# Recurrence products of a hybrid two-layer block on Trainium2: grouped by the array's form, with zero-padded 128-row operands for scores, low-rank parts and gate rows

## The chip, the cores and the metric

The kernel runs on one core of a Trainium2 chip. The metric is the device time of one execution in microseconds (us), lower is better. Engines are named as in the profile: PE is TensorE (matmuls), PEld its weight loads, DVE is VectorE, ACT is ScalarE, POOL is GpSimd, and SP issues DMAs.

## What is computed

Two layers with the same structure work on 512 tokens of width 1024: 256 context tokens and 256 latent ones. Each layer is a half-weight SwiGLU feed-forward part, a mixing part, and another feed-forward part, each behind a modulated norm. The mixing part has three branches, whose outputs are gated, projected and summed:

```python
z = h @ W_in                      # one projection, columns split among the branches
y_m = mLSTM(...)                  # 4 heads, 64-wide q and k: scores q k^T times exp(decay), both directions
y_r = RWKV7(...)                  # 8 heads of 64 channels, both directions
y_a = differential_attention(...) # 4 heads, each with two 64-wide q/k maps
x  += gate2 * W_o(sum_b sigmoid(g_b) * (y_b @ P_b))
```

The recurrent branch (RWKV-7) keeps a 64x64 state per head and direction. With decay w, removal a, key k, value v and read-out r, the state goes through S <- S diag(w) + (S a) b^T + v k^T at each token, and y = S r. The kernel computes it in chunks of 64 tokens. Within a chunk the values u of the removal term solve a triangular system, (I - A) u = X, where X has a part from the values of the chunk (Ma times v) and a part from the state (S a).

## The kernel before

Tokens lie on the free axis of feature-major tiles; a matmul works on 128 features and up to 512 tokens. Weights come from DRAM as 512 KB units (`unit`, L130), which ACT and DVE split into a leading and a trailing half (`hi`, `lo`), and each dense product is the sum of three passes, seen in the rows as `hh,hi`, `hl,hi` and `hh,lo`. Their PSUM tiles are called `m` and `d`.

The mixing part of a layer interleaves two programs. The recurrent branch runs at high priority in four tiles t = 0 to 3 of two heads each. For each tile there is `rwkv_stage1` (elementwise work and the low-rank products `lora`, L904 to 910), `rwkv_stage2` (the products A inside the chunks, L976 to 980, and transposes), `rwkv_solve` (the inverses: a chain on DVE and 32x32 products sG and sB on PE) and `rwkv_chain` (L1090 to 1161). The other program is the generator `mixers`: attention (`attn_rot`, `attn_head`), the mLSTM (`mlstm_steps`) and the merge, whose dense products fill PE between the recurrent steps. Tables (`BUDGET`, `GATES`) say how much of it goes between the columns of the recurrent tiles. The order of instructions on each engine is set when the program is built, by a scheduler that looks at priorities and at when operands are ready. PSUM has eight banks in four tags: two for `d`, three for `m` (scores too), two for `c` (the recurrent products A, X, U, S, Y) and one for `s` (low-rank products).

The chain takes eight steps. Each handles one forward and one backward chunk (d = 0, 1) of two heads (h = 0, 1), head h on partitions 64h to 64h + 63. In a step: X is four products of Ma with UV and four of ar with the state S (L1102 to 1107); DVE copies X; U is four products with the inverses Bt (L1116); DVE and ACT copy U into UV; the new state's S is four products of BK with UV (L1128), and DVE adds and scales it (L1157, L1158); and Y, by `out()` one step later, is four pairs of a product of UV with Mr and one of the state with ar (L1135 to 1137), which DVE adds to `ry` or ACT copies there. Steps i = 1 to 7 have the state products, except where both chunks are context chunks in layer 1, whose Y isn't needed.

By its operands a matmul uses a part of the array, and the profile prints that after its operands. The local product of Y (UV with Mr) contracts 128 rows into 64 columns: 128\*64. The state product (S with ar) contracts the 64 rows of a head: 64\*64. A (L980), the attention scores (L592), the mLSTM's scores (L746) and the trailing parts of the low-rank weights (L907) contract 64 rows into 128 columns: 64\*128. For the scores, two heads' or two maps' 64 features share a 128-partition tile `qkT` or `mqk`, and each product takes its half of it.

The mLSTM's gate rows lie in two 64-row tiles, `gi` and `Fc`, each with four transposes of 64 rows (L705 to 708).

Of the kernel before, what the change touches and what calls it, by code (L numbers as in the profile page):

```python
# [35 lines left out]
# columns of the packed per-partition parameters  # L36
# [3 lines left out]
# columns of the packed constants  # L40
# [10 lines left out]
# per layer: gate tiles after each attention and mLSTM head; other work (in us of TensorE) before and after  # L51
# the columns of each next recurrent tile
# [24 lines left out]
SPLIT = 16  # L77

class Halves:
    """a unit's 1024 columns in two tiles"""
# [9 lines left out]
class Builder:  # L92
# [36 lines left out]
    def unit(self, spec):  # L129
        """hi and lo parts of a unit; exact together"""  # L130
# [31 lines left out]
    def fm_tile(self, spec, lo=0, h=None, ps=None):  # L162
        """one feature-major tile of 128 columns: PSUM [128 cols, tokens]"""
# [17 lines left out]
    def fm_first(self, units, pss, parts):  # L181
        """the first tiles after a norm: every feature block goes to all of them as soon as it is there"""
# [25 lines left out]
    def ada_first(self, i, j):  # L208
        """block j of modulation vector i (0 shift, 1 scale) of the first norm, on TensorE"""
# [18 lines left out]
    def ada_first_shift(self, j):  # L228
        """the shift on VectorE"""
# [13 lines left out]
    def load_c(self, after=lambda: None):  # L243
        """silu of the two condition vectors on every partition"""
# [23 lines left out]
    def ada_steps(self):  # L268
        """the others on VectorE: one block of 128 outputs at a time"""
# [27 lines left out]
    def sqrt_ahead(self):  # L297
        """has ScalarE's table for the square roots of the next norm loaded before they are due"""
# [4 lines left out]
    def sumsq(self, k, c):  # L303
        """adds the squares of x_k to the running sum of these tokens"""
# [9 lines left out]
    def norm_stats(self, parts):  # L314
        """1 / rms of these tokens on every partition, in PSUM"""
# [16 lines left out]
    def norm_apply(self, l, i, k, psr, parts):  # L332
        """feature block k of the modulated norm, split into hi and lo"""
# [12 lines left out]
    def norm_mod(self, l, i, parts):  # L346
        """norm and modulation of these tokens"""
# [5 lines left out]
    def x_update(self, l, gi, k, ps, c):  # L353
        """x_k += 0.5 * gate * ps"""
# [75 lines left out]
    def conv(self, out, ps, w, lo=0):  # L430
        """out = centred 3-tap convolution of ps; w: three [128,1] taps"""
# [11 lines left out]
    def attn_prep(self):  # L443
# [21 lines left out]
        self.qg, self.nl, self.subw = qg, nl, sub  # L465

    def tm_group(self, cols, consume, t0=0):
        """token-major product with 256 columns (cols: (c0, width) ranges): PSUM [128 tokens, 256]
        for each of the token tiles from t0 on"""
# [19 lines left out]
    def attn_qk(self, h):  # L489
        """raw q and k of a head, token-major (token tile, q or k), and the sums of their squares"""  # L490
# [14 lines left out]
    def attn_qk_pair(self, hp):  # L505
        """the same for two heads without the context's q: slots k0 k1 q2 k2 q3 k3 of the token tiles"""
# [32 lines left out]
    def attn_rot(self, qkr, ss):  # L539
        """normalised and rotated q and k of a head, feature-major"""  # L540
# [29 lines left out]
        for w in range(2):  # L570
# [4 lines left out]
            o = a.tile([P, NT], F32, name="qkT", tag="qkT", bufs=4)  # L575
            nc.scalar.copy(o[:, t0 * P :], pt[:, t0 * P :])
# [3 lines left out]
    def attn_head(self, hp, h, qT, kT, v):  # L580
# [3 lines left out]
        for i in range(lo // P, 4):  # L584
# [60 lines left out]
    def mlstm_steps(self):  # L645
# [4 lines left out]
        def qk(c0, ti, lo):  # L650
# [5 lines left out]
            o = a.tile([P, NT], F32, name="mqk", tag="mqk", bufs=4)  # L656
            nc.vector.scalar_tensor_tensor(o[:, lo:], th[:, lo:], 1.0, z[:, lo:], op0=ALU.add, op1=ALU.mult)
            return o

        q, k = [], []  # L660
# [3 lines left out]
        for i in range(2):  # L664
            k.append(qk(O_MK + P * i, 2 + i, 0))
            yield 5
# [3 lines left out]
        gi = a.tile([64, NT], F32, name="gi", tag="P00", bufs=1)  # L670
# [24 lines left out]
        # m = F + G; em = exp(-m); nG = -G, its hi part on the first half of the partitions, lo on the other  # L695
        nc.vector.tensor_tensor(Fc, Fc, G, op=ALU.add)
# [7 lines left out]
        for t in range(4):  # L704
            self.tr(pt[:, t * 64 : t * 64 + 64], gi[:, t * P : (t + 1) * P], 64)  # L705
        for t in range(4):
            self.tr(pt[:, 256 + t * 64 : 256 + t * 64 + 64], Fc[:, t * P : (t + 1) * P], 64)
        used = lambda x: x.rearrange("p (t d r) -> p (t d) r", t=4, d=2)[:, :, 0:4]
        nc.scalar.copy(ac.rearrange("p t (d r) -> p (t d) r", d=2), used(pt[:, :256]))
        nc.scalar.activation(em.rearrange("p t (d r) -> p (t d) r", d=2), used(pt[:, 256:]), AF.Exp, scale=-1.0)  # L710
# [5 lines left out]
        for h in range(4):  # L716
            if h % 2 == 0:
# [9 lines left out]
                yield 10  # L727
            ps = self.fm_tile(self.blocks("w_in", l, O_MO + h * P), lo)
            tho = a.tile([P, NT], F32, name="tho", tag="tho", bufs=1)
            nc.scalar.activation(tho[:, lo:], ps[:, lo:], AF.Tanh, scale=0.5)  # L730
            r = slice(64 * (h % 2), 64 * (h % 2) + 64)
            qt, kt = q[h // 2], k[h // 2]
            # s-block j: scores against the query tokens it can reach
# [9 lines left out]
            for j in range(4):  # L743
                s0 = max(lo, 0 if j < 2 else CTX)
                pS = self.psm("mS")
                self.mm(pS[:, s0:], kt[r, j * P : (j + 1) * P], qt[r, s0:], True, True)  # L746
                for d in range(2):
                    # reachable query blocks
# [66 lines left out]
    def rwkv_small(self):  # L815
# [6 lines left out]
        # hi and lo parts of a direction on the two halves of the partitions  # L822
# [4 lines left out]
        for src, dst in ((tw, self.tw), (pa, self.ta)):  # L827
            for d in range(2):
                r, o = slice(64 * d, 64 * d + 64), slice(64 - 64 * d, 128 - 64 * d)
                nc.scalar.copy(dst[r, d], src[r])  # L830
                nc.vector.tensor_tensor(dst[o, d], src[r], dst[r, d].bitcast(F32), op=ALU.subtract)
        self.vpad = a.tile([P, 128 + NT], F32, name="vpad", tag="vpad", bufs=1)
# [22 lines left out]
    def rwkv_cols(self, t):  # L855
# [12 lines left out]
        ll = a.tile([P, 2, P], F32R, name="loral", tag="loral", bufs=1)  # L868
        nc.scalar.copy(lh, lw)
        for d in range(2):  # L870
            r = slice(64 * d, 64 * d + 64)
            nc.vector.tensor_tensor(ll[r], lw[r, d::2], lh[r, d::2].bitcast(F32), op=ALU.subtract)
# [9 lines left out]
    def rwkv_stage1(self, t, r, k, v, lw, g2):  # L882
        """everything that is elementwise over (channel, token)"""
# [5 lines left out]
        # normalised keys  # L889
# [5 lines left out]
        # 1 / max(norm, 1e-12)  # L895
# [7 lines left out]
        for d in range(2):  # L903
            rows = slice(64 * d, 64 * d + 64)  # L904
# [663 lines left out]
```

## Time and profile before

| what | value |
|---|---|
| time, median of 3 runs | 2867.44 us (2856.05 to 2876.06) |
| profiled execution: span, the one time that the page gives of it | 2880.2 us |
| PE busy | 2784.9 us, 97% |
| DVE busy | 1862.6 us, 65% |
| ACT busy | 1146.1 us, 40% |
| POOL busy | 236.5 us, 8% |
| mixing stage of layer 0 | about 430 to 1195 us |
| mixing stage of layer 1 | about 2040 to 2600 us |

Busy time is the time in which at least one instruction of the engine is under way. On PE successive matmuls overlap, so in a timeline the cost of a piece is read from its start to the next piece's start, not from its own duration. A float32 product leaves two records, a transpose or a product of split halves one. The granted clock (PEclk) is a share of full speed.

### The profile page before, as it was taken

The page shows a single profiled execution, that of the slowest core. Times are in us where ns is not written, and L with a number is a line of the kernel's source. Part 1 is how long each engine was busy: PE and PEld are TensorE (multiplying, and loading weights), DVE is VectorE, ACT ScalarE, POOL GpSimd, SP SyncE. Part 2 cuts the span into 40 slices and gives each one's busy share as a digit, 9 for nine tenths or more (in the row PEclk, how much of TensorE's full clock was granted, in tenths as well). Part 3 has the DMA queues.
Part 4 walks back from the last instruction along what each step waited for, and adds up shares of the span by engine and source line. Part 5 has one row for each costly group of instructions (what it writes and reads, how often), then busy time and mean ns, then how long its engine had stood idle before and what let it go on. Part 6 is the DMA issues. An engine that isn't in the chain of part 4 may idle for free.

```text
span 2880.2 us, 43519 instructions
## 1 busy us (share of the span) xinstructions
PE 2784.9 (97%) x17198; PEld 2280.8 (79%) x17198; DVE 1862.6 (65%) x3611; ACT 1146.1 (40%) x1955; POOL 236.5 (8%) x330
## 2 busy tenths in 40 slices
PE   7999999999999999999999999999999899998999
PEld 5888887668676677688888888888878677878999
DVE  7999368474593663589995443333877677746654
ACT  3322244443553543343222332222554546444543
POOL 0000002111110200200000000000212121112000
PEclk9999999799997999999999999999989899989999
DMA  7777322111121222666773232222221121226454
GB/s 264 237 238 227 100 94 68 34 63 39 59 75 41 70 74 80 225 205 221 237 240 109 88 102 96 95 95 74 98 78 57 61 65 57 92 92 214 162 183 147
DMA packets 102432, 349.65 MB, mean 121 GB/s; under 512 B 13362, under 2 KB 17842, under 8 KB 101972
## 3 DMA queue, kind: packets, MB, share of 16 engines
q1 hardware_dynamic: 91872, 315.10, 33.5%
q0 software_dynamic: 9024, 31.60, 3.3%
q8 instruction: 135, 2.21, 0.3%
q14 instruction: 69, 0.57, 0.1%
q10 hardware_dynamic: 1332, 0.18, 0.0%
HBM read 327.82 MB, written 19.01 MB: 120 GB/s over the span
## 4 chain that ended last, share of the span: by engine, by line
PE 60%; DVE 8%; issue 4%; ACT 3%; DMA 2%; POOL 1%; DVEq 0%; POOLq 0%; ACTq 0%; SPq 0%
PE d L102 25%; PE m L102 22%; PE Y L102 2%; PE A L102 2%; DVE lo L144 1%; PE X L102 1%; DVE op L1038 1%; DVE T L1041 1%; DMA yin<-yd 1%; DMA raw<-in_ws 1%; PE mo L102 1%; PE aS L102 1%; PE S L102 1%; PE U L1116 1%; ACT hi L140 1%
## 5 line engine op out<-in xcount | busy, mean ns | idle before, releaser
L140 ACT CAST hi<-raw 128x1024 fp32r<-128x1024 f32 x430 | 451.0, 1049 | 1022.0 <-PE m L102 468.0
L144 DVE TENSOR_TENSOR lo<-raw,hi 128x1024 fp32r<-128x1024 f32 (+1 forms) x508 | 544.6, 1076 | 322.7 <-ACT hi L140 315.6
L102 PE MATMUL m<-hh,hi 128*128 128x512 f32 (+1 forms) x1440 | 510.8, 357 | 3.9 <-ACT hh L342 2.5
L102 PE MATMUL m<-hl,hi 128*128 128x512 f32 (+1 forms) x1440 | 513.2, 357 | 0.0
L102 PE MATMUL m<-hh,lo 128*128 128x512 f32 (+1 forms) x1440 | 512.5, 357 | 0.0
L102 PE MATMUL d<-hh,hi 128*128 128x256 f32 (+1 forms) x976 | 357.5, 367 | 4.0 <-DVE x L359 2.7
L102 PE MATMUL d<-hl,hi 128*128 128x256 f32 (+1 forms) x976 | 353.1, 362 | 0.4 <-DVE hl L196 0.4
L102 PE MATMUL d<-hh,lo 128*128 128x256 f32 (+1 forms) x976 | 349.1, 358 | 0.1
L239 DVE SCALAR_TENSOR_TENSOR ajunk<-araw,scb 128x1024 f32<-128x1024 f32 x272 | 332.5, 1222 | 5.1 <-ACT scb L266 0.5
L102 PEld LDWEIGHTS m<-hh,hi 128*128 128x128 f32 x1440 | 272.0, 190 | 45.3 <-ACT hh L342 3.1
L102 PEld LDWEIGHTS m<-hh,lo 128*128 128x128 f32 x1440 | 272.8, 190 | 40.2 <-DVE lo L144 0.2
L102 PEld LDWEIGHTS m<-hl,hi 128*128 128x128 f32 x1440 | 272.8, 190 | 39.9 <-issue 0.2
L102 PE MATMUL d<-ul,hi 128*128 128x512 f32 (+1 forms) x770 | 269.3, 350 | 0.0
L102 PE MATMUL d<-uh,hi 128*128 128x512 f32 (+1 forms) x770 | 268.5, 349 | 0.0
L102 PE MATMUL d<-uh,lo 128*128 128x512 f32 (+1 forms) x770 | 268.3, 349 | 0.0
L102 PEld LDWEIGHTS d<-hh,hi 128*128 128x128 f32 x976 | 191.9, 197 | 37.5 <-issue 8.2
L102 PEld LDWEIGHTS d<-hl,hi 128*128 128x128 f32 x976 | 191.7, 196 | 34.5 <-issue 12.7
L102 PEld LDWEIGHTS d<-hh,lo 128*128 128x128 f32 x976 | 191.9, 197 | 26.3 <-issue 5.1
L102 PEld LDWEIGHTS d<-uh,hi 128*128 128x128 f32 x770 | 145.1, 188 | 20.8
L102 PEld LDWEIGHTS d<-ul,hi 128*128 128x128 f32 x770 | 145.4, 189 | 19.7
L102 PEld LDWEIGHTS d<-uh,lo 128*128 128x128 f32 x770 | 144.9, 188 | 19.9
L102 PE MATMUL d<-lo,hh 128*128 128x256 f32 x480 | 142.9, 298 | 0.0
(357 smaller groups left out, 4268.3 us busy)
## 6 DMA issues: line engine op xcount, KB each, us to landing
raw<-in_ws SPq DMA_DIRECT2D x430, 512.0 KB, 3.4
araw<-in_ws SPq DMA_DIRECT2D x146, 512.0 KB, 4.4
gd<-gth POOLq DMA_DIRECT2D x24, 256.0 KB, 2.5
gth<-gd SPq DMA_DIRECT2D x24, 256.0 KB, 2.9
xd<-x POOLq DMA_DIRECT2D x2, 2048.0 KB, 7.9
gd<-gth POOLq DMA_DIRECT2D x24, 128.0 KB, 2.0
gth<-gd SPq DMA_DIRECT2D x24, 128.0 KB, 3.3
yin<-yd POOLq DMA_DIRECT2D x11, 256.0 KB, 4.6
```

Of the source, the lines that this page charges most:

```text
L102: self.nc.tensor.matmul(out, lhsT=lhsT, rhs=rhs, start=start, stop=stop)
L140: self.nc.scalar.copy(hi, raw)
L144: self.nc.vector.tensor_tensor(lo[:, c], raw[:, c], hi[:, c].bitcast(F32), op=ALU.subtract)
L239: self.nc.vector.scalar_tensor_tensor(junk, raw, 1.0, self.scb[:, st], op0=ALU.mult, op1=ALU.mult, accum_out=self.mods[l][:, s, k, st : st ...
L1038: nc.vector.tensor_tensor(w, A[:, i + 1 :, i : i + 1].broadcast_to(w.shape), T[:, i : i + 1, c].broadcast_to(w.shape), op=ALU.mult)
L1041: nc.vector.tensor_tensor(t, t, w, op=ALU.add)
L1116: self.nc.tensor.matmul(pu[ur, d * 64 : d * 64 + 64], lhsT=Bt[hr, 8 * d + cs[d]], rhs=X[hr, d], start=True, stop=True, tile_position=(hr.s ...
```

## The change

The diff does six things.

1. Attention scores: q of a head goes into `qz`, a tile with a slot of 512 columns for each of the two maps; the other map's 64 rows are zeros, set once per layer on POOL. Each score contracts 128 rows. ACT copies q in two halves instead of one piece. `qkT` has 2 buffers instead of 4, `qz` one.
2. The mLSTM's k likewise goes into `mkz`, of which there is one; it is filled by two half-tile operations on DVE, and the second pair of heads gets its k when it is due, no longer at the start.
3. The gate rows lie in one 128-row tile `gf`, with four 128x128 transposes per layer instead of eight of 64 rows.
4. The trailing parts of the low-rank weights lie in a tile with zeros in the other direction's rows, and the product contracts 128 rows.
5. A: both heads' banks are allocated together, and the source alternates heads.
6. The chain: in X the state products of both heads come first, then the UV products. Y gets a bank in `c` for d = 0 and the bank of `s` for d = 1. Its four local products follow S directly, and its four state products with the evacuation are issued together after the X of the next step (`y_state`).

The core of the diff (comments that go and unchanged lines are left out):

```diff
@@ attn_rot
-            o = a.tile([P, NT], F32, name="qkT", tag="qkT", bufs=4)
-            nc.scalar.copy(o[:, t0 * P :], pt[:, t0 * P :])
+            if w == 0:
+                o = self.qz[self.nq % QZ[l]]
+                self.nq += 1
+                for m in range(2):
+                    mr = slice(64 * m, 64 * m + 64)
+                    nc.scalar.copy(o[mr, m, t0 * P :], pt[mr, t0 * P :])
+            else:
+                o = a.tile([P, NT], F32, name="qkT", tag="qkT", bufs=2)
+                nc.scalar.copy(o, pt)
@@ attn_head
-                r = slice(64 * m, 64 * m + 64)
-                self.mm(pS[:, : nk * P], qT[r, i * P : (i + 1) * P], kT[r, : nk * P], True, True)
+                self.mm(pS[:, : nk * P], qT[:, m, i * P : (i + 1) * P], kT[:, : nk * P], True, True)
@@ rwkv_stage1, lora
-                self.mm(ps, lw[1][rows, i], x[rows, d], False, True)
+                self.mm(ps, lw[1][:, 2 * i + d], x[:, d], False, True)
@@ rwkv_stage2
+                pAs = [self.psc("A") for _ in range(2)]
+                for n in range(4):
+                    c = 4 * g + n
+                    for h in range(2):
+                        hr = slice(64 * h, 64 * h + 64)
+                        self.mm(pAs[h][:, n * P : (n + 1) * P], bk[hr, c].rearrange("p a b -> p (a b)"),
+                                ar[hr, d, c].rearrange("p a b -> p (a b)"), True, True)
@@ rwkv_chain
+        def y_state(py, cs, S):
+            if S is not None:
+                for d in range(2):
+                    for h in range(2):
+                        hr = slice(64 * h, 64 * h + 64)
+                        self.mm(py[d][hr, :64], S[hr, d], ar[hr, d, cs[d], 1], False, True)
...
                 c = cs[d]
+                if i:
+                    for h in range(2):
+                        hr = slice(64 * h, 64 * h + 64)
+                        self.mm(px[hr, d * 64 : d * 64 + 64], ar[hr, d, c, 0], S[hr, d], True, False)
                 for h in range(2):
                     hr = slice(64 * h, 64 * h + 64)
-                    self.mm(px[hr, d * 64 : d * 64 + 64], Ma[hr, d, c], UV[hr, c, h], True, i == 0)
-                    if i:
-                        self.mm(px[hr, d * 64 : d * 64 + 64], ar[hr, d, c, 0], S[hr, d], False, True)
+                    self.mm(px[hr, d * 64 : d * 64 + 64], Ma[hr, d, c], UV[hr, c, h], i == 0, True)
...
-                py = self.psc("Y")
+                py = [self.psc("Y"), self.pss("Y")]
                 for d in range(2):
                     for h in range(2):
                         hr = slice(64 * h, 64 * h + 64)
-                        self.mm(py[hr, d * 64 : d * 64 + 64], UV[:, c, h], Mr[:, d, c, h], True, i == 0)
-                        if i:
-                            self.mm(py[hr, d * 64 : d * 64 + 64], S[hr, d], ar[hr, d, c, 1], False, True)
+                        self.mm(py[d][hr, :64], UV[:, cs[d], h], Mr[:, d, cs[d], h], True, i == 0)
```

How the order of instructions moves is shown at three places. First PE, in a step of the chain near the end of layer 0's mixing part (t = 3). U, S, X and Y are the recurrent products and d is dense filler. The rows of before:

```order
L102 MATMUL S<-UV,BK 64x64 x4
L102 MATMUL X<-UV,Ma 64x64
L102 MATMUL d<-hl,hi 128x512
L102 MATMUL d<-hh,lo 128x512
L102 MATMUL Y<-Mr,UV 64x64
L102 MATMUL Y<-ar,S 64x64
L102 MATMUL X<-S,ar 64x64
...
L102 MATMUL Y<-Mr,UV 64x64
L102 MATMUL Y<-ar,S 64x64
L102 MATMUL d<-hh,hi 128x512
L1116 MATMUL U<-X,Bt 64x64 x4
```

The rows of the change at the same place:

```order
L1161 MATMUL U<-X,Bt 64x64 x4
L103 MATMUL d<-hh,hi 128x512
L103 MATMUL d<-hl,hi 128x512
L103 MATMUL d<-hh,lo 128x512
L103 MATMUL S<-UV,BK 64x64 x4
L103 MATMUL Y<-Mr,UV 64x64 x4
L103 MATMUL Y<-ar,S 64x64 x4
L103 MATMUL d<-hh,hi 128x512
L103 MATMUL X<-S,ar 64x64 x2
L103 MATMUL X<-UV,Ma 64x64 x2
L103 MATMUL X<-S,ar 64x64 x2
L103 MATMUL X<-UV,Ma 64x64 x2
```

Before, a lone X product stood behind S, and Y's pairs stood between X and U; now X is in one piece, and Y stands ahead of it, in two runs.

Second PE at products A of one tile in layer 0, with the numbers of the buffers: A_5458 and A_5466 are the banks of head 0 and head 1. Before:

```order
L102 MATMUL A_5458<-ar_5451,bk_4674 128x128 x4
L102 MATMUL d_4985<-hh_99,lo_4982 128x512
L102 MATMUL d_4985<-hh_99,hi_4981 128x512
L102 MATMUL d_4985<-hl_100,hi_4981 128x512
...
L102 MATMUL A_5466<-ar_5451,bk_4674 128x128 x4
```

The same place in the change, where A_5468 and A_5469 are the two banks:

```order
L103 MATMUL A_5468<-ar_5461,bk_4684 128x128 x4
L106 MATMUL qkT_4865<-idt_73,qkr_4733 128x128 x2
L106 MATMUL qkT_4872<-idt_73,qkr_4733 128x128 x2
L103 MATMUL d_5029<-hh_99,lo_5026 128x512
L103 MATMUL d_5029<-hh_99,hi_5025 128x512
...
L103 MATMUL A_5469<-ar_5461,bk_4684 128x128 x4
```

The heads still stand in runs of four products of one head, though the source alternates them.

Third DVE, in the chain: S is the state, `ry` the sum of Y. Before:

```order
L1157 TENSOR_TENSOR S<-S 128x128
L1158 TENSOR_TENSOR S<-S,eC 128x128
L1111 COPY X<-X 128x128
L1143 TENSOR_TENSOR ry<-ry,Y 128x64 x2
L1121 COPY UV<-U 64x2x64
```

One of the steps in the change where the order differs most:

```order
L1193 TENSOR_TENSOR S<-S 128x128
L1134 TENSOR_TENSOR ry<-ry,Y 128x64
L1194 TENSOR_TENSOR S<-S,eC 128x128
L1134 TENSOR_TENSOR ry<-ry,Y 128x64
L604 TENSOR_REDUCE mx<-aS 128x1
L1156 COPY X<-X 128x128
```

An addition of Y stands between the two operations of the state here; in most steps both additions stand behind them.

## Rows read from the trace of the kernel before

**Rows 1.** Page, part 1: engine, busy us (share of span), instructions.
```profile
PE 2784.9 (97%) x17198; PEld 2280.8 (79%) x17198; DVE 1862.6 (65%) x3611; ACT 1146.1 (40%) x1955; POOL 236.5 (8%) x330
```

**Rows 2.** Windows by stage: busy us by engine, then PEclk, DMA share, GB/s.
```profile
430.00:1195.00 765.00, 734.37 (x4814) 549.15 (x4813) 458.69 (x1034) 334.55 (x660) 104.61 (x132) 0.93 0.21 69
...
2040.00:2600.00 560.00, 537.01 (x4234) 434.84 (x4233) 394.54 (x965) 284.65 (x552) 93.51 (x133) 0.92 0.23 73
```

**Rows 3.** Windows of the five low-clock stretches: the longest, and their sum.
```profile
871.10:908.50 37.40, 37.40 (x258) 24.05 (x258) 9.33 (x29) 12.88 (x39) 0.68 (x2) 0.50 0.07 22
...
sum 129.30, PE 129.30 PEld 89.93 DVE 34.23 ACT 49.70 POOL 5.95; mean PE 25.86 PEld 17.99 DVE 6.85 ACT 9.94 POOL 1.19
```

**Rows 4.** Timeline of PE, start of the longest one: start us, us, engine, operation.
```profile
871.05 0.90 PE L1067 MATMUL sG<-Rt,Z 32*32 32x32 f32 x13
```

**Rows 5.** Timeline of PE around a low-rank product, layer 0.
```profile
775.43 0.39 PE L102 MATMUL d<-hl,hi 128*128 128x512 f32 x1
775.66 0.40 PE L102 MATMUL lw<-tws,lorah 128*128 128x512 f32 x1
775.98 0.50 PE L102 MATMUL lw<-tws,loral 64*128 64x512 f32 x1
776.42 0.44 PE L105 MATMUL amT<-idt,ae 128*128 128x128 f32 x2
```

**Rows 6.** Timeline of PE, a chain step of layer 0's last tile.
```profile
1084.63 0.45 PE L1116 MATMUL U<-X,Bt 64*64 64x64 f32 x8
...
1085.91 0.45 PE L102 MATMUL S<-UV,BK 128*64 128x64 f32 x8
1086.29 0.33 PE L102 MATMUL X<-UV,Ma 64*64 64x64 f32 x2
1086.55 0.50 PE L102 MATMUL d<-hl,hi 128*128 128x512 f32 x1
...
1087.47 0.27 PE L102 MATMUL Y<-ar,S 64*64 64x64 f32 x1
...
1088.13 0.33 PE L102 MATMUL Y<-Mr,UV 128*64 128x64 f32 x2
...
1089.67 0.51 PE L102 MATMUL d<-hh,hi 128*128 128x512 f32 x1
1090.10 0.45 PE L1116 MATMUL U<-X,Bt 64*64 64x64 f32 x8
```

**Rows 7.** Groups by line and form, PE: busy us, mean ns, idle before.
```profile
L102 PE MATMUL Y<-ar,S 64*64 64x64 f32 x352 | 57.6, 244 | 0.0
```

**Rows 8.** Timeline of PE: a lone score, two adjacent ones, a full-row float32 product.
```profile
726.57 1.12 PE L102 MATMUL aS<-qkT 64*128 64x512 f32 x2
727.62 0.71 PE L102 MATMUL ay<-am,av 128*128 128x128 f32 x4
...
2250.45 1.13 PE L102 MATMUL aS<-qkT 64*128 64x512 f32 x4
2251.51 0.38 PE L102 MATMUL d<-hl,hi 128*128 128x256 f32 x1
...
787.14 1.02 PE L102 MATMUL gm<-ry,cst 128*128 128x512 f32 x2
...
788.23 0.39 PE L102 MATMUL d<-hl,hi 128*128 128x512 f32 x1
```

**Rows 9.** Timeline of PE, products A of both heads in one run, layer 0.
```profile
619.96 1.71 PE L102 MATMUL A<-ar,bk 64*128 64x128 f32 x16
```

**Rows 10.** Timeline of DVE in the chain step of rows 6.
```profile
1086.73 0.29 DVE L1158 TENSOR_TENSOR S<-S,eC 128x128 f32<-128x128 f32 x1
1088.23 0.29 DVE L1111 COPY X<-X 128x128 f32<-128x128 f32 x1 [1.21 <-PE X L102]
1089.77 0.35 DVE L1143 TENSOR_TENSOR ry<-ry,Y 128x64 f32<-128x64 f32 x2 [1.25 <-PE Y L102]
```

**Rows 11.** Waits by line, whole span: us in total, times, longest.
```profile
ACT ry L1145 <- PE Y L102: 75.3, 22, 6.6
```

More of the change, by code (lines that the diff above doesn't have):

```diff
@@ L77 @@
 SPLIT = 16
+QZ = (1, 1)
 class Halves:
@@ L465, in attn_prep @@
         self.qg, self.nl, self.subw = qg, nl, sub
+        self.qz, self.nq = [a.tile([P, 2, NT], F32, name="qz", tag=f"qz{i}", bufs=1) for i in range(QZ[l])], 0
+        for t in self.qz:
+            nc.gpsimd.memset(t, 0.0)
     def tm_group(self, cols, consume, t0=0):
@@ L655, in qk @@
             nc.scalar.activation(th[:, lo:], z[:, lo:], AF.Tanh, scale=0.5)
-            o = a.tile([P, NT], F32, name="mqk", tag="mqk", bufs=4)
-            nc.vector.scalar_tensor_tensor(o[:, lo:], th[:, lo:], 1.0, z[:, lo:], op0=ALU.add, op1=ALU.mult)
+            if ti < 2:
+                o = a.tile([P, NT], F32, name="mqk", tag="mqk", bufs=2)
+                nc.vector.scalar_tensor_tensor(o[:, lo:], th[:, lo:], 1.0, z[:, lo:], op0=ALU.add, op1=ALU.mult)
+                return o
+            o = kz
+            for n in range(2):
+                r = slice(64 * n, 64 * n + 64)
+                nc.vector.scalar_tensor_tensor(o[r, n], th[r], 1.0, z[r], op0=ALU.add, op1=ALU.mult)
             return o
-        q, k = [], []
+        q = []
         for i in range(2):
@@ L663, in mlstm_steps @@
             yield 5
-        for i in range(2):
-            k.append(qk(O_MK + P * i, 2 + i, 0))
-            yield 5
+        kz = a.tile([P, 2, NT], F32, name="mkz", tag="mkz", bufs=1)
+        nc.gpsimd.memset(kz, 0.0)
+        qk(O_MK, 2, 0)
+        yield 5
         pg = self.fm_tile([("w_gate", l, kk * P, 0, P) for kk in range(KT)])
         gb = pv[:, PV_GB : PV_GB + 1]
-        gi = a.tile([64, NT], F32, name="gi", tag="P00", bufs=1)
+        gf = a.tile([P, NT], F32, name="gf", tag="P00", bufs=1)
+        gi = gf[0:64]
         fb = a.tile([64, NT], F32, name="fb", tag="m2", bufs=3)
@@ L694, in mlstm_steps @@
         scans(G, gi, ALU.max, -1e30)
-        nc.vector.tensor_tensor(Fc, Fc, G, op=ALU.add)
+        nc.vector.tensor_tensor(gf[64:128], Fc, G, op=ALU.add)
         GS = a.tile([P, NT], F32R, name="GS", tag="Gc", bufs=1)
@@ L704, in mlstm_steps @@
         for t in range(4):
[L705 to L710, printed above, removed]
+            self.tr(pt[:, t * P : (t + 1) * P], gf[:, t * P : (t + 1) * P])
+        used = lambda i: pt.rearrange("p (t i d r) -> p t i d r", t=4, i=2, d=2)[:, :, i, :, 0:4]
+        as4 = lambda x: x.rearrange("p t (d r) -> p t d r", d=2)
+        nc.scalar.copy(as4(ac), used(0))
+        nc.scalar.activation(as4(em), used(1), AF.Exp, scale=-1.0)
         yield 5
@@ L831, in rwkv_small @@
                 nc.vector.tensor_tensor(dst[o, d], src[r], dst[r, d].bitcast(F32), op=ALU.subtract)
+        self.ll = a.tile([P, 4, P], F32R, name="loral", tag="loral", bufs=1)
+        nc.gpsimd.memset(self.ll.bitcast(F32), 0.0)
         self.vpad = a.tile([P, 128 + NT], F32, name="vpad", tag="vpad", bufs=1)
@@ L867, in rwkv_cols @@
         lh = a.tile([P, 4, P], F32R, name="lorah", tag="lorah", bufs=1)
-        ll = a.tile([P, 2, P], F32R, name="loral", tag="loral", bufs=1)
+        ll = self.ll
         nc.scalar.copy(lh, lw)
@@ L1097, in rwkv_chain @@
         S = pending = None
+        def y_state(py, cs, S):
[4 more added lines that the diff above has]
+                        self.mm(py[d][hr, :64], S[hr, d], ar[hr, d, cs[d], 1], False, True)
+            for d in range(2):
+                c = cs[d]
+                if c in seen:
+                    nc.vector.tensor_tensor(y[:, c], y[:, c], py[d][:, :64], op=ALU.add)
+                else:
+                    nc.scalar.copy(y[:, c], py[d][:, :64])
+                    seen.add(c)
         for i in range(8):
@@ L1118, in rwkv_chain @@
             st = cs[1] - cs[0]
-            both = (lambda x: x[:, cs[0] :: st][:, 0:2]) if st > 0 else (lambda x: x[:, cs[0] :: st][:, 0:2])
+            both = lambda x: x[:, cs[0] :: st][:, 0:2]
             pu2 = pu[:, :128].rearrange("p (d x) -> p d x", d=2)
@@ L1128, in rwkv_chain @@
                         self.mm(pS[hr, d * 64 : d * 64 + 64], BK[:, d, cs[d], hr], UV[:, cs[d], h], True, True)
-            def out(i=i, cs=cs, S=S):
-                if cs[0] < lc and cs[1] < lc:
-                    return
-                py = self.psc("Y")
+            if not (cs[0] < lc and cs[1] < lc):
+                py = [self.psc("Y"), self.pss("Y")]
                 for d in range(2):
-                    c = cs[d]
                     for h in range(2):
                         hr = slice(64 * h, 64 * h + 64)
-                        self.mm(py[hr, d * 64 : d * 64 + 64], UV[:, c, h], Mr[:, d, c, h], True, i == 0)
-                        if i:
-                            self.mm(py[hr, d * 64 : d * 64 + 64], S[hr, d], ar[hr, d, c, 1], False, True)
-                for d in range(2):
-                    c = cs[d]
-                    if c in seen:
-                        nc.vector.tensor_tensor(y[:, c], y[:, c], py[:, d * 64 : d * 64 + 64], op=ALU.add)
-                    else:
-                        nc.scalar.copy(y[:, c], py[:, d * 64 : d * 64 + 64])
-                        seen.add(c)
-            pending = out
+                        self.mm(py[d][hr, :64], UV[:, cs[d], h], Mr[:, d, cs[d], h], True, i == 0)
+                if i:
+                    pending = lambda py=py, cs=cs, S=S: y_state(py, cs, S)
+                else:
+                    y_state(py, cs, None)
             if i < 7:
@@ L1159, in rwkv_chain @@
                 S = Sn
-        pending()
+        if pending:
+            pending()
         return t, y, g2, bon
```

19 lines of the change are left out of this document (8 added, 11 removed).

## The prediction

> **What bounds the kernel now.** I read the engine table of the page first. TensorE (PE) is busy for 97% of the 2880.2 us span [rows 1], so a change pays by what it takes out of PE's own sequence, as long as nothing else then comes late. The windows by stage come second. The change acts only in the two mixing stages, 430 to 1195 us (layer 0) and 2040 to 2600 us (layer 1). There PE is busy 734.37 of 765 us and 537.01 of 560 us: 54 us of idle time in all. VectorE (DVE) is busy 459 and 395 us, ScalarE (ACT) 335 and 285 us [rows 2]. So even there PE is the bound, and the other engines have room. The mean granted clock of these stages is 0.93 and 0.92 [rows 2]. Five stretches of 129.30 us in all ran at 0.50, the 1.2 GHz level, with PE busy throughout [rows 3]; the longest begins within a run of 32x32 products of the solve [rows 4].
>
> The timeline of PE comes third, since "busy" hides what matters here. PE runs matmuls in forms (rows x columns of the array): dense filler in 128\*128, X, U and Y's state part in 64\*64, S and Y's local part in 128\*64, A and scores in 64\*128. I read costs as the distance from one start to the next. A dense product follows its like after 0.23 us (775.43 to 775.66); when another form follows, the distance is 0.32 (775.66 to 775.98), so a switch costs about 0.09 [rows 5]. Three dense products between two other forms then take 3 x 0.23 + 2 x 0.09 = 0.87, and one 0.32. In a step of the chain, eight records of one form, heads in turn, take 0.38 us (S, 1085.91 to 1086.29; four matmuls, for each leaves two records). One matmul alone between other forms takes 0.26 (X, 1086.29 to 1086.55). The Y part alternates between its two forms at each matmul: three pairs take 1.54 us (1088.13 to 1089.67), 0.51 a pair, and the four pairs of a step 2.05. A whole step, from U to the next U, is 5.47 us (1084.63 to 1090.10) [rows 6].
>
> **The change part by part.**
>
> *Y.* There are 352 records of Y's state part [rows 7]; at eight a step, 44 steps have it. The order shows 176 alternations before; now the four local products stand behind S, of the same form, and the four state products are one run. The run of 8 products of 64\*64 (seven of X, one of Y) took 0.66 us (1087.47 to 1088.13) against 0.38 for 4, so a matmul more in a run is worth 0.07: 4 x 0.07 = 0.28 for the local part. The state part is a run of its own: 0.38. So 2.05 becomes 0.66, and 44 x 1.39 = 61. In 25 of the steps before, as at 1087.47, the first state product already stood in X's run, which made it 0.26 - 0.07 = 0.19 cheaper: 61 - 5 = **56 us**. Some of the local products are split between S products in the new order, but these are of one form and cost no switch.
>
> *X.* The order has 56 places where one X product on UV stood alone between dense products; all are in the run now. 56 x (0.26 - 0.07) = **11 us**.
>
> *Low-rank parts.* A 64-row low part takes 0.44 us to the next start, and the product ahead of it 0.32 instead of 0.23 [rows 5]. Full-row it should follow like a dense one: 0.44 + 0.32 - 2 x 0.23 = 0.30, and 32 of them give **10 us**.
>
> *Scores.* A lone 64-row score over 512 keys takes 1.05 us (726.57 to 727.62), and entering it 0.09. I have no full-row score; the nearest row is a full-row float32 product of 512 columns, 1.09 us with one dense product in it (787.14 to 788.23), so 0.86 by itself [rows 8]. A lone one then gains 1.05 + 0.09 - 0.86 = 0.28. But two scores that stand side by side use the two row halves: the pair took 1.06 us (2250.45 to 2251.51) [rows 8], hardly more than one. Padded, such a pair costs 2 x 0.86 and loses 1.72 - 1.06 - 0.09 = 0.57; a pair of 256 keys loses about 0.2, an estimate by half the width. By the order, 30 attention scores stood alone, 4 pairs were of 512 and 5 of 256: 30 x 0.28 - 4 x 0.57 - 5 x 0.2 = 5. The mLSTM's 32 scores stood in some 25 runs: 25 x 0.28 = 7. Together **12 us**.
>
> [...]
>
> *A.* The source now alternates heads, which could let the two row halves overlap as in the score pair. One run of both heads, 16 records, takes about 1.7 us [rows 9]. But the order still shows four products of one head, then (often after dense work) four of the other; I count only 6 runs that mix heads. Half of 1.6 in 6 runs is 5; I take **4 us**. Bounds: 0, and 16 x 1.6 = 26 if all 32 were mixed.
>
> *Gate rows* go from 8 small transposes a layer to 4: under 1 us. *Zero fills* on POOL, once per layer, and the halved copies (8 more q copies on ACT, 4 more k products on DVE, a few tenths of a us each): nothing, hidden behind engines that are idle for 30% or more of these stages [rows 2]; without that cover some 5 us.
>
> The counted total is 56 + 11 + 10 + 12 + 4 = **93 us**.
>
> **What comes late next.** With Y gone from between X and U, X's copy has less cover. Before, it began 0.10 us after the X run and took 0.29 (1088.23) [rows 10], while Y held PE until 1089.67. Now three dense products stand there, 0.87 us: still enough. The new step is U 0.38, three dense 0.87, S with Y 0.66, Y's state part 0.38, one dense 0.32, X 0.66, three dense 0.87: 4.1 us against 5.47. S is scaled 1.11 us after it starts (1085.91 to 1086.73 + 0.29) [rows 10]; X now follows it after 0.66 + 0.38 + 0.32 = 1.36: 0.25 us of slack. In 10 of 48 steps the new order of DVE puts the first of Y's two adds (0.35 for both [rows 10]) ahead of S's scaling. That add needs the state part, 1.04 after S, so the scaling ends near 1.04 + 0.10 + 0.18 + 0.29 = 1.6, some 0.25 too late: 10 x 0.25, about 3 us. Half of the small gains of scores and low-rank parts (22 us) stand just before a wait for ACT or DVE, whose work doesn't shrink: I charge 5. So **85 us** net. The profiled execution would be 2880.2 - 85 = 2795 us. The median of the runs shown is 12.8 us below that execution's span, so the same 85 us taken from 2867.44 give **2782 us**.
>
> **The rivals.**
>
> 1. *The gain is partly absorbed.* Each solve is a chain on DVE that dense work covers; if that work is done 93 us sooner, PE waits at the solves and in the last steps of layer 1, where no filler is left. For it: the 54 us of idle time in these stages [rows 2] show that cover already runs out somewhere. Against it: DVE is 60 to 70% busy there. With half lost, 2867 - 46 = 2821; I give 2810 to 2850.
>
> 2. *The clock comes back too.* The stretches at 0.50 [rows 3] might shorten when chain and filler become dense full-array work. If half of the 129.30 us ran at the 2.4 GHz level, it would take 32 us instead of 65: 2867 - 85 - 32 = 2750, and down to 2715 if more of it does. Against it: they begin at the solves, which the change leaves alone.
>
> 3. *Slower: Y's banks hold up U.* The step's PSUM banks rotate between two; before, Y's bank was next wanted by S, now Y's first bank is next wanted by U, and Y holds it from S until its evacuation. By the new step, Y is complete 1.04 us after S starts, the adds behind S's scaling end near 1.5, and U follows S after 0.66 + 0.38 + 0.32 + 0.66 + 0.87 = 2.9: slack 1.4 us. PE works in order, so a late evacuation blocks the dense work behind U as well. The total turns into a loss when evacuation is later by 1.4 + 93/44 = 3.5 us in every step; at 5 us late it costs 44 x 3.6 = 158 against the 93: 2867 + 65 = 2932 us. Against it: where ACT evacuates Y, it waited 75.3 us for it in 22 waits [rows 11], so it mostly stands ready; a delay of 3.5 us would need several long instructions ahead of each evacuation.
>
> 4. *A's alternation isn't done.* The order shows that; it is in the sum at 4 us.
>
> 5. *Padding loses at the scores.* If the scheduler's lone scores gave no gain and all 24 attention pairs (16 of 512 keys, 8 of 256) had run at the pair's price of [rows 8], padding them would cost 16 x 0.57 + 8 x 0.2 = 11 us instead of bringing 5: 2782 + 16 = 2798. Against it: by the order only 9 pairs stand together.
>
>
> **How the numbers follow.** My forecast, 2755 to 2794, has a chance of 0.52; rival 5 (2794 to 2810) 0.05; partial absorption (2810 to 2850) 0.20; the clock (2715 to 2755) 0.15; the slower case 0.04; anything else, near no change, 0.04. The likeliest gives 2782. The range 2715 to 2830 takes in the first, the score case, the clock, and about half of the absorbed case: 0.82. About 1% (29 us) is what a measurement here can tell from no change. Faster than 2839: 0.52 + 0.05 + 0.15, and 0.15 of the absorbed case: 0.87. Within 1%: 0.05 + 0.04 = 0.09. Slower: 0.04.
>
> **What the changed profile would show.** Y's state products in runs of eight records with about 0.38 us to the next start, and local ones beside S. U to U at about 4.1 us at full clock in layer 0's last tile. Low parts at 0.23 and full-row scores at 0.86 us from start to start. PE's idle time in the mixing stages near 54 to 62 us; if it grows by 40 or more, rival 1 holds. Mean clock over 0.95 there would mean rival 2. PE idle before U, released by an evacuation of Y, would mean rival 3. I am wrong in the sum if the step stays above 5 us although Y's alternation is gone, or if full-row scores cost what the 64-row ones did.

## The result, and the profile after

The changed kernel takes 2787.3 us (median of 4 runs, 2785.19 to 2790.99) against 2871.22 us before: a ratio of 0.9704, 95% interval 0.9665 to 0.9742. That is 84 us less, where 85 were forecast. Its profiled execution took 2785.32 us with a span of 2783.6, so span against span it is 96.6 us below the kernel before. The first row of its page and its row of cores:

```profile
PE 2643.5 (95%) x17190; PEld 2204.9 (79%) x17190; DVE 1866.8 (67%) x3615; ACT 1152.2 (41%) x1965; POOL 242.9 (9%) x336
```

```profile
core 0: 2783.6 us, clock 0.978
```

PE is busy 141 us less than in [rows 1], which is more than the span lost: idle time of PE has grown from 95 to 140 us. And the mean granted clock rose; the row of before is

```profile
core 0: 2880.2 us, clock 0.962
```

I use these three numbers for every run below. Busy time times clock is the work at full clock; busy time times (1 - clock) is what the clock cost; span less busy time is idle. Each line is one profiled execution. The last column is the clock of all the executions on record of that kernel, and it shows how far one line can be from the next execution: 0.01 of clock is about 28 us, and the profiled execution of e2 is the slowest of its five.

| kernel | span | PE busy | clock | work | lost to the clock | idle | clock, all executions |
|---|---|---|---|---|---|---|---|
| before | 2880.2 | 2784.9 | 0.962 | 2679 | 106 | 95 | 0.960 to 0.971 |
| changed | 2783.6 | 2643.5 | 0.978 | 2585 | 58 | 140 | 0.973 to 0.978 |
| changed, second time (e5) | 2790.3 | 2652.6 | 0.974 | 2584 | 69 | 138 | 0.972 to 0.979 |
| chain alone (e1) | 2816.9 | 2700.4 | 0.965 | 2606 | 95 | 117 | 0.964 to 0.968 |
| full-row operands alone (e2) | 2860.6 | 2752.7 | 0.965 | 2656 | 96 | 108 | 0.965 to 0.980 |
| changed without part 5 (e6) | 2770.8 | 2648.1 | 0.979 | 2593 | 56 | 123 | 0.978 to 0.982 |
| changed with 64-row scores (e4) | 2781.3 | 2658.6 | 0.978 | 2600 | 59 | 123 | 0.978 to 0.982 |
| 64-row scores, without part 5 (e7) | 2793.8 | 2670.6 | 0.975 | 2604 | 67 | 123 | 0.965 to 0.975 |

So by the mean clock the work fell by 94 us, the loss to the clock by 48, and idle time grew by 45. The mean clock charges PE's busy time with slow time in which PE was idle. With the clock of each stretch instead, the work is 2677 before and 2591 in the changed kernel, 86 us less where 93 were counted, and the loss to the clock fell by 55.

Span times clock leaves work and idle time together, and it can be had for every execution. Its medians are 2772 to 2774 us before, 2717 in the changed kernel, 2718 in e1, 2771 in e2, 2714 in e6, 2721 in e4 and 2717 in e7. So all kernels of this table with the regrouped chain are alike in it, within 7 us; what sets their times apart is mostly the clock.

The chain step of layer 0's last tile, to be set against [rows 6] (PE timeline: start, us, operation):

```profile
1012.90 0.45 PE L1161 MATMUL U<-X,Bt 64*64 64x64 f32 x8
...
1014.17 0.45 PE L103 MATMUL S<-UV,BK 128*64 128x64 f32 x8
1014.45 0.40 PE L103 MATMUL Y<-Mr,UV 128*64 128x64 f32 x8
1014.79 0.45 PE L103 MATMUL Y<-ar,S 64*64 64x64 f32 x8
1015.16 0.49 PE L103 MATMUL d<-hh,hi 128*128 128x512 f32 x1
1015.59 0.33 PE L103 MATMUL X<-S,ar 64*64 64x64 f32 x4
...
1016.20 0.50 PE L103 MATMUL d<-hl,hi 128*128 128x512 f32 x1
...
1017.09 0.45 PE L1161 MATMUL U<-X,Bt 64*64 64x64 f32 x8
```

U to U is 4.19 us (5.47 before). S with Y's local part takes 0.62, Y's state part 0.37 and X 0.61, where 0.66, 0.38 and 0.66 were forecast. A full-row score of 512 keys takes 0.86 us to the next start, and a full-row low part 0.24 (0.86 and 0.23 forecast):

```profile
618.22 1.02 PE L103 MATMUL aS<-qkT,qz 128*128 128x512 f32 x2
619.08 0.61 PE L103 MATMUL ay<-am,av 128*128 128x128 f32 x4
...
747.85 0.40 PE L103 MATMUL la<-tas,loral 128*128 128x512 f32 x1
748.09 0.39 PE L103 MATMUL d<-hl,hi 128*128 128x512 f32 x1
```

The idle time has three main places (waits by line, whole span: us, times, longest):

```profile
PE gv L103 <- ACT gsq L1211: 19.7, 7, 4.4
PE m L103 <- ACT yh L196: 18.1, 8, 5.2
PE la L103 <- ACT w L937: 13.8, 5, 5.9
```

In the trace of before the same three were

```profile
PE m L102 <- ACT yh L195: 6.2, 4, 2.4
PE gv L102 <- ACT gsq L1174: 4.0, 2, 2.4
PE la L102 <- ACT w L914: 2.1, 1, 2.1
```

so they hold 39 of the 45 us. One of them in the timeline of all engines:

```profile
580.44 3.27 POOL L964 TENSOR_TENSOR bk<-kd,L 64x512 f32<-64x512 f32 x2 [0.82 <-DVE kd L959]
...
583.75 0.63 ACT L1211 ACTIVATE gsq<-ry 128x512 f32<-128x512 f32 x1 [2.13 <-POOL bk L964]
...
584.43 1.55 PE L103 MATMUL gv<-gsq,cst 128*128 128x512 f32 x2 [4.05 <-ACT gsq L1211]
```

`gsq`, the squares for the group norm of the tile that is done, lies in the buffer that the next tile's keys `kd` use; ACT waits until POOL has read them, and PE waits for ACT, 4.05 us here, with all its further products queued behind `gv`.

### The profile page after: what moved, and what is told of

The parts are those of the page before. It is cut to its first block, busy times and chain, and to the rows that moved or that the text cites. A ratio compares the mean times of both kernels' runs of the same rounds, so it can differ in the third digit from the quotient of the medians.

```text
span 2783.6 us, 43578 instructions
## 1 busy us (share of the span) xinstructions
PE 2643.5 (95%) x17190; PEld 2204.9 (79%) x17190; DVE 1866.8 (67%) x3615; ACT 1152.2 (41%) x1965; POOL 242.9 (9%) x336
## 4 chain that ended last, share of the span: by engine, by line
PE 77%; DVE 10%; issue 4%; ACT 4%; DMA 2%; POOL 2%; DVEq 0%; ACTq 0%; POOLq 0%; SPq 0%
PE d L103 32%; PE m L103 32%; PE A L103 2%; DVE lo L145 2%; PE X L103 1%; DMA yin<-yd 1%; DVE op L1064 1%; PE Y L103 1%; PE S L103 1%; DVE T L1067 1%; PE U L1161 1%; PE aS L103 1%; PE mo L103 1%; PE ay L103 1%; DVE bk L965 1%
## 5 line engine op out<-in xcount | busy, mean ns | idle before, releaser
L103 PE MATMUL d<-hh,hi 128*128 128x512 f32 (+1 forms) x976 | 352.9, 362 | 7.4 <-DVE x L360 2.4
L103 PE MATMUL d<-hh,lo 128*128 128x512 f32 (+1 forms) x976 | 348.4, 357 | 0.5 <-DVE lo L145 0.5
L103 PE MATMUL d<-hl,hi 128*128 128x512 f32 (+1 forms) x976 | 346.6, 355 | 0.0
L103 PE MATMUL d<-hi,hh 128*128 128x256 f32 x480 | 141.0, 294 | 1.8 <-ACT hi L141 1.7
```

What stands on the lines that cost most here:

```text
L103: self.nc.tensor.matmul(out, lhsT=lhsT, rhs=rhs, start=start, stop=stop)
```

## The experiments

**The two halves alone.** e1 is the kernel before with part 6 only; e2 is the kernel before with parts 1 to 4 only.

```diff
# e1: rwkv_chain as changed, the rest as before
-                self.mm(px[hr, d * 64 : d * 64 + 64], Ma[hr, d, c], UV[hr, c, h], True, i == 0)
+                self.mm(px[hr, d * 64 : d * 64 + 64], Ma[hr, d, c], UV[hr, c, h], i == 0, True)
-            py = self.psc("Y")
+            py = [self.psc("Y"), self.pss("Y")]
# e2: qz, mkz, gf and the padded loral as changed, the rest as before
-                self.mm(ps, lw[1][rows, i], x[rows, d], False, True)
+                self.mm(ps, lw[1][:, 2 * i + d], x[:, d], False, True)
```

> Only the chain's regrouping (part 6), on the kernel before: X's products in one run, Y's local products behind S, its state products in one run, two banks for Y. Form theory (a gain is the switches and lone products taken out, priced from start to start): in the changed kernel's trace Y, X and S cost 68 us less than before when weighted by the granted clock, so 2871 - 68 = 2803 us, and the rest of the gain is the scores' and low-rank parts'. Clock theory (a good part of the gain is that the half-speed stretches vanish): the time-weighted loss to the clock falls from 108 us by 30 or more here too, and the mean granted clock goes from 0.962 to 0.97 or more; about 2771 unless idle time eats it. Absorption theory: PE's idle time grows by 30 or more, 2830 us or above.

e1 took 2815.55 us against 2867.25 before: 0.9817 (0.9783 to 0.985), 52 us less. Its work is 73 us below that of before (69 with the clock of each stretch), as the form theory has it with 68; idle time took 21 back, and the profiled clock gave 11. The form theory's time (2803) is missed by 13 us; the clock theory's and the absorption theory's conditions are not met (clock 0.965, idle up by 21, not 30). Over all executions on that chip the clock gave nothing: the median of span times (1 - clock) is 92 us before and 96 in e1.

> Only the full-row operands (scores of attention and mLSTM, low-rank parts, gate rows), without the chain and without A. Form theory: 20 us less work (mLSTM scores 7, attention scores 5, low-rank parts 8), 2871 - 20 = 2851 us. Packing rival (padding loses where two scores could share the rows): scores cost as much or more, 2865 us or more. Clock theory: if full-row products hold the clock up, more than 30 us gained and a mean clock of 0.97 or more.

e2 took 2844.26 us: 0.9909 (0.9876 to 0.9941), 23 us less. The packing rival's 2865 us or more is out for scores and low-rank parts as a whole. The work is 23 us less (20 with the clock of each stretch, as forecast), but that it equals the time is chance. Over all executions span times clock is 2 us below that of before, and the median loss to the clock fell from 92 to 71 us. So the work that padding saved came back as idle time, and what e2 gained is almost all the clock's. The work of the two halves adds up: 73 + 23 = 96, where both together took 94. The clock's loss fell by 11 and 10 us in the two profiles and by 48 in that of both together; over all executions on this chip it fell by nothing in e1, by 21 in e2, and by 35 in e3 below, which has both halves without part 5.

Windows over the same two stretches behind the solves of tile 2 and tile 0 in layer 0, where the kernel before ran at 0.50 [rows 3], show where the clock differs (span, busy us by engine, then PEclk, DMA share, GB/s). Chain alone, full-row operands alone, changed kernel, then the two kernels with 64-row scores and all other parts (e4) or all but part 5 (e7):

```profile
843.00:881.00 38.00, 38.00 (x323) 25.62 (x319) 12.65 (x43) 14.32 (x43) 1.61 (x4) 0.60 0.07 22
512.00:543.00 31.00, 31.00 (x280) 21.12 (x279) 11.30 (x26) 13.44 (x34) 1.67 (x4) 0.67 0.08 26
```

```profile
864.00:902.00 38.00, 38.00 (x459) 28.34 (x458) 19.86 (x68) 17.11 (x57) 1.94 (x5) 1.00 0.13 43
511.00:542.00 31.00, 31.00 (x335) 21.34 (x335) 15.72 (x33) 19.74 (x44) 3.68 (x7) 1.00 0.08 27
...
664.00:702.00 38.00, 38.00 (x233) 28.95 (x233) 7.66 (x21) 7.21 (x16) 0.00 (x0) 0.51 0.08 29
```

```profile
828.00:866.00 38.00, 38.00 (x523) 28.43 (x522) 21.84 (x73) 19.44 (x60) 2.33 (x5) 1.00 0.16 49
508.00:539.00 31.00, 30.98 (x397) 21.59 (x398) 15.02 (x40) 17.95 (x40) 2.06 (x5) 1.00 0.08 27
```

```profile
832.00:870.00 38.00, 38.00 (x438) 26.88 (x436) 18.14 (x60) 18.59 (x57) 1.91 (x5) 0.87 0.08 24
507.00:538.00 31.00, 31.00 (x399) 21.47 (x397) 15.56 (x40) 19.85 (x44) 2.20 (x6) 1.00 0.08 27
```

```profile
835.00:873.00 38.00, 37.39 (x412) 25.40 (x413) 16.89 (x58) 16.43 (x53) 2.07 (x5) 0.82 0.07 24
513.00:544.00 31.00, 30.93 (x396) 21.43 (x395) 14.80 (x38) 18.53 (x41) 2.07 (x5) 1.00 0.08 27
```

With the chain alone regrouped these 69 us still ran at 0.60 and 0.67; with the full-row operands they ran at 1.00. But full-row scores are not what it takes: e4 and e7 have 64-row scores, and with full-row low-rank parts and gate rows and the regrouped chain they ran at 1.00 behind tile 0 and at 0.87 and 0.82 behind tile 2. And e2, with Y's alternation left in place, has a new slow stretch (664 to 702), which begins within Y's alternating products. Which of the parts keeps the clock up is not isolated here.

**Part 5 undone.** e3 and e6 are the changed kernel with A's banks allocated and filled head by head, as before.

```diff
-                pAs = [self.psc("A") for _ in range(2)]
+                for h in range(2):
+                    pA = self.psc("A")
```

> The changed kernel without part 5: A's two banks are allocated and filled head by head again. If the scheduler undoes the alternation (the order shows four products of one head in a run either way), the time is that of the changed kernel, 2787 us, within 5. If alternation pays, 2791 to 2805.

> The changed kernel once more, so that the next three stand beside it on the same chip: 2787 us, within 5.

> The changed kernel without part 5 (A's banks allocated and filled head by head), beside the changed kernel. Theory: with both banks of the recurrent products reserved for A at once, PE stands idle before A (9.6 us there in the changed kernel, 6.0 without part 5, 5.0 before the change), and this moves what follows; 8 to 14 us faster than the changed kernel. Rival: the 14 us seen between two different chips are none of part 5's; within 4 us of it.

e3 took 2773.64 us (0.9668, 0.9635 to 0.9701), on another chip than the changed kernel. Beside it on one chip, e6 took 2768.76 us (2767.0 to 2772.8; ratio 0.9628, 0.9597 to 0.9659) and the changed kernel (e5) 2792.57 (2776.38 to 2798.47; 0.9698, 0.9663 to 0.9734). So part 5 costs 24 us, more than the 8 to 14 expected, and the kernel without it beats both. The place that I had named is wrong, though: PE's wait for `bk` before A, the largest there, is 6.4 us in e5 and 5.9 in e6. Between the two profiles e6 has 15 us less idle time and loses 13 less to the clock, against 9 more of work; over all executions the clock has 20 of the 24 us (a median loss of 73 and 53). The idle time is spread (before `gv` 22.6 against 18.1, before `la` 13.8 against 10.6, before `sG` 5.0 against 2.0).

**A's second bank from elsewhere.** e8 is the changed kernel with

```diff
-                pAs = [self.psc("A") for _ in range(2)]
+                pAs = [self.psc("A"), self.psm("A")]
```

> The changed kernel with the second bank of A taken from the three banks of the dense tiles and scores instead of the two of the recurrent products. In the order 48 neighbouring products of A then change heads instead of 28. If the wait for a bank is what part 5 costs, idle time before A falls from 9.6 us to 5 or less, and the time to 2775 to 2781. If alternating heads overlap in the row halves, a run of 16 alternating records takes 0.85 to 1.1 us instead of 1.6, some 6 us more gained. If neither, 2787.

e8 took 2784.79 us (0.9682, 0.9652 to 0.9713): between the two, and its interval overlaps that of e5. The idle time before A rose to 14.4 us instead of falling, so the bank theory has no support. What it shows is the price of alternation where it is really done. A whole tile's direction in one run, then two runs of one head in e6 at the same place; both ran at a granted clock of 0.50:

```profile
460.06 5.43 PE L103 MATMUL A<-ar,bk 64*128 64x128 f32 x32 [2.69 <-DVE bk L965]
465.42 1.11 PE L106 MATMUL bkT<-idt,bk 128*128 128x128 f32 x4
```

```profile
465.56 2.07 PE L103 MATMUL A<-ar,bk 64*128 64x128 f32 x8
...
468.29 2.07 PE L103 MATMUL A<-ar,bk 64*128 64x128 f32 x8
```

32 records take 5.4 us with heads that partly alternate where four such runs of one head would take 4 x 2.07 = 8.3: they do overlap. Part of the difference is the shorter runs; the 16-record run of f2 below, at 0.50 and with one head after the other, takes 3.3, so 6.5 for 32. In e8 as a whole the work of A fell from 65 to 59 us, by the 6 forecast.

**Scores of 64 rows again.** e4 is the changed kernel, e7 the kernel without part 5, both with packed q and k in attention and mLSTM.

```diff
-                self.mm(pS[:, : nk * P], qT[:, m, i * P : (i + 1) * P], kT[:, : nk * P], True, True)
+                self.mm(pS[:, : nk * P], qT[r, i * P : (i + 1) * P], kT[r, : nk * P], True, True)
```

> The changed kernel with the attention and mLSTM scores contracting 64 rows again, no zero-padded q and k. Form theory: 12 us more, 2799 us. Packing rival: 2787 or less.

> The changed kernel without part 5 and with 64-row scores in attention and mLSTM: the chain, the low-rank parts and the gate rows alone are left. Form theory for the scores: 9 to 12 us slower than the kernel without part 5 alone. Packing rival: as fast or faster than that kernel.

e4 took 2778.03 us (0.9682, 0.9646 to 0.9718), not to be told from the changed kernel's ratio; by its time alone the packing rival (2787 or less) would hold. e7 took 2802.92 (0.974, 0.9709 to 0.9772), 34 us more than e6 on the same chip. The work is 15 and 11 us above that of the full-row twin (10 and 7 with the clock of each stretch), near the forecast 12, but the times differ by anything from about -15 to +34. Of the 34, the clock has 31 (median losses of 84 and 53 us). That full-row scores take less work is settled; what the kernel gains depends on the idle time and the low clock of each new order.

**The covered waits taken away.** f1 puts `gsq` in the room of `Ma`, which is dead by then; f2 also puts the gates `aa` in the room of `Z`. f3 and f4 make both moves in the kernel before and in the changed one.

```diff
-GSQ = "tmp"
+GSQ = "Ma"
-            aa = T2("aa", "w")
+            aa = T2("aa", "Z")
```

> The kernel without part 5 (2769 us), with the squares of the group norm (gsq) in the room of Ma, which is dead by then, instead of the buffer that the next tile's keys (kd) also use. Theory: what PE won in the chain it lost at waits that Y's slow part had covered; PE stood idle 18.1 us before gv for gsq, and gsq waited on POOL's and DVE's bk, the readers of kd. The idle time before gv falls below 6 us and the time by 8 to 14 us, to about 2758. Rival: the wait only moves to the next instruction; 2765 to 2775.

> The same, and the removal gates aa in the room of Z (dead after the solve) instead of the buffer of the decays w, so that w of the second direction needn't wait for the first direction's bk. Theory: the 10.6 us before la, waiting for w, go too: about 2748 us. Rival: the scan into L, which has one buffer for both directions, waits for bk in w's place, and nothing more is gained; as f1.

> The kernel before the change with the same two moves of rooms. Theory: there PE waited only 4.0 us before gv and 2.1 before la, for Y's alternation gave cover; so at most 6 us are gained, within 1% of before. Rival (the two waits cost the kernel before as much, by way of ACT and DVE): 15 us or more gained.

> The changed kernel, with part 5, and the same two moves. Theory: 36 us of idle time before gv and la fall to 10, so some 20 to 25 us faster than the changed kernel: about 2768. If part 5's loss of some 20 us sits in these waits, it comes out beside f2; if it sits elsewhere, it stays 15 us or more above f2.

Three of the four missed. f1 took 2781.87 us (0.9683, 0.9659 to 0.9707), f2 2797.14 (0.9734, 0.971 to 0.9758), f4 2805.4 (0.9754, 0.9727 to 0.9781): slower than the kernels they were made from by 13, 28 and 13 us, between chips. f3 took 2884.55 (1.0036, 1.0013 to 1.0058), within the 1% forecast for it, but 11 us slower, where up to 6 less were expected. The named waits did go. Groups of e6, then of f1 (busy us, mean ns, idle before and its releasers):

```profile
L103 PE MATMUL A<-ar,bk 64*128 64x128 f32 x512 | 74.3, 295 | 7.2 <-DVE bk L965 5.9 <-ACT BK L1012 0.6 <-DVE Mr L1006 0.4
L103 PE MATMUL gv<-gsq,cst 128*128 128x512 f32 x8 | 7.2, 1004 | 10.3 <-ACT gsq L1208 10.3
L103 PE MATMUL gv<-gsq,cst 128*128 128x256 f32 x8 | 3.3, 502 | 7.8 <-ACT gsq L1208 7.8
```

```profile
L103 PE MATMUL A<-ar,bk 64*128 64x128 f32 x512 | 84.5, 325 | 20.5 <-DVE bk L965 11.7 <-DVE Mr L1006 6.0 <-ACT gsq L205 1.4
L103 PE MATMUL gv<-gsq,cst 128*128 128x512 f32 x8 | 4.1, 592 | 0.0
L103 PE MATMUL gv<-gsq,cst 128*128 128x256 f32 x8 | 2.9, 454 | 1.1 <-ACT gsq L1208 1.1
```

Idle time before `gv` fell from 18.1 to 1.1 us, that before A rose from 7.2 to 20.5, and all idle time went from 123 to 126 us. Of these 20.5, 11.7 are for `bk`, the last product of DVE and POOL ahead of A: the wait removed ahead of A came back at A. Part of the new wait is of my making: A's results go to `Ma`'s room, which `gsq` now holds, in f2 until DVE has scaled `ry`:

```profile
PE A L103 <- DVE ry L1217: 17.8, 4, 7.6
PE A L103 <- DVE Mr L1006: 12.3, 6, 5.4
```

The loss in time of all three is the clock's: in f2 0.966 instead of 0.979, 91 us lost to it instead of 56. Span times clock is even 3, 11 and 12 us lower in f1, f2 and f4 than in the kernels that they were made from (medians). One place of it, where A follows an idle stretch; the 16 records take 3.3 us, 1.7 in [rows 9]:

```profile
2281.98 3.26 PE L103 MATMUL A<-ar,bk 64*128 64x128 f32 x16 [7.63 <-DVE ry L1217]
```

So a test of these rooms without a new holder was not made, and whether a shorter `bk` chain would free the 40 us stays open.

## Why the prediction was right, and where its steps were not

For the steps on PE I add up, for each matmul of a trace, the distance to the next start less idle time, weighted by the granted clock of the stretch that it stands in.

*Y and X: right.* Y and S together (S runs straight into Y now) went from 116 to 62 us, 54 less; 56 were forecast. X went from 51 to 37, 14 less against 11. e1 has the same numbers without the other parts. The step from U to U is 4.19 us against 4.1.

*Low-rank parts and scores: right.* With the products ahead of them, low-rank products went from 25 to 17 us, 8 less against 10; scores from 58 to 46, 12 less against 12. The Trainium skill, "TensorEngine Tiling (Array Packing)", section "When to Use Tiling", gives 2x row tiling for a contraction of 64 rows. For two scores that stand together the trace agrees (1.06 us for both, 1.05 for a lone one [rows 8]); most stood alone here, and padded they took 12 us less work, so rival 5 is out.

*A: wrong.* The alternation was not done, as the order showed, so its own work stayed at 65 us. But I priced the part at a gain of 4 us by its work alone. e5 and e6 show a loss of 24 us. The step that failed is "Bounds: 0, and 16 x 1.6 = 26 if all 32 were mixed": the lower bound allowed for no loss, though the part reserves both banks of the recurrent products at once and changes the order of what follows. Which of these costs the 24 us is not settled.

*What comes late next: far too small.* I charged 3 us for Y's add and 5 for waits; idle time grew by 42 to 45. In the two mixing stages it grew from 54 us to 98 (702 less 659.39, and 557 less 501.45):

```profile
429.00:1131.00 702.00, 659.39 (x4868) 512.55 (x4868) 471.72 (x1044) 340.19 (x667) 112.67 (x139) 0.98 0.25 80
1983.00:2540.00 557.00, 501.45 (x4348) 423.90 (x4348) 397.57 (x973) 285.59 (x554) 109.60 (x151) 0.93 0.27 86
```

That is 44 more, and by the prediction's own sign (40 or more) rival 1 holds. I had looked at waits inside the step (there the slack held: PE's idle time before U is 2.5 us and before X 0.9 in the whole changed kernel, and none before U is released by an evacuation of Y, so rival 3 is out), and not at those between tiles:

```profile
L1161 PE MATMUL U<-X,Bt 64*64 64x64 f32 x512 | 33.3, 235 | 2.5 <-DVE X L1156 1.3 <-ACT Bt L1113 1.2
L103 PE MATMUL X<-S,ar 64*64 64x64 f32 x448 | 32.1, 233 | 0.9 <-DVE ry L1134 0.6 <-DVE S L1194 0.4
```

`gv`, `la` and the branch inputs `yh` hang on DVE, POOL and ACT, which are about as busy as before (DVE 1866.8 and 1862.6 us), while PE has less work to stand above them. That this missing cover is the cause is argued, not shown: f1, f2 and f4 took waits away and gained no time. Of rival 1's places the solves don't show it (PE waits 5.4 us there, 5.1 before); the last part of layer 1 does, with most of the wait for `yh` (13.1 us, of 128x256), and the group norm and the gates of the next tile come on top.

*The clock: rival 2 came true in part.* The loss to it fell by 37 to 48 us in the profiles, and by 33 from median to median on e5's chip; my rival had 32 for half of [rows 3]'s stretches, with a chance of 0.15, and these are 129 of the 217 us that the trace of before has at 0.50. The argument against it failed: "they begin at the solves, which the change leaves alone". The change left the solves alone, and yet e2, e4 and e7 ran at 0.82 to 1.00 behind them: what stands behind the solve counts too.

So 2782 was met at 2787 partly by luck: idle time took some 45 us where 8 were charged, and the clock, for which the sum had nothing, gave about as much back. The work term, which the sum was about, is right to 7 us: 93 were counted, and 86 fell away in the profiled execution (54 + 14 + 8 + 12 = 88 by the parts above).

## What to carry to other kernels

Price an array's switches from start to start and count them in the built order: that sum held here to a few us, part by part. Then ask of every later wait what PE work had been covering it, between stages as well as inside the loop, and compare granted clocks over several executions, for the clock of one profile can be the odd one. Where a program orders instructions by a scheduler, a part that changes little work can still move the time by 1%, so such parts are to be timed alone.

## What was not expected of the hardware

Idle time alone does not tell the granted clock. PE was busy for at least 37.39 of the 38 us behind tile 2's solve in all the kernels shown; the granted clock there was 0.50 in [rows 3]'s stretch, 0.60 with the regrouped chain, 0.82 and 0.87 in the kernels with 64-row scores that have the chain, the low-rank parts and the gate rows changed, and 1.00 in e2 and in the changed kernel, whose scores are full-row too. The same program varies as well: 0.965 to 0.980 over the five executions of e2, which is 28 us (2834.64 to 2862.35).
